# The first of eight column groups of a two-branch decoder layer takes three of its sixteen chunk pairs by seven block products instead of eight

## The chip, the cores and the metric

The kernel runs on one core of one Trainium2 chip. The metric is the device time of one execution in microseconds (us). The kernel before was timed three times: 1829.57, 1831.45 and 1831.59 us, median 1831.45.

## The reference

One layer, in fp32, on 256 tokens with 16 learned meta tokens ahead of them (272 rows of 4096):

```python
h = rmsnorm(x, norm_g)
p = h @ w_in                     # 4096 x 16384: q k v g_attn | b c h_conv z, 2048 columns each
o = stick_breaking_attention(heads(q), heads(k), heads(v))      # 16 heads of 128
o = group_rmsnorm(o * silu(g_attn), attn_norm_g, 16)
y = b_conv * short_conv(c_conv * h_conv, conv_w)                # width 3 along the positions
y = group_rmsnorm(y * silu(z_conv), conv_norm_g, 16)
hs = x + concatenate([o, y]) @ w_out                            # 4096 x 4096
return rmsnorm(hs, final_norm_g)[:, 16:]                        # the meta tokens are dropped
```

## The kernel before, in words

**Operands in two halves.** Every fp32 operand is split into a rounded high part and the rest: ScalarE (ACT) casts it (line 308, tiles `wh`), VectorE (DVE) subtracts (line 309, tiles `wl`). A block product on TensorE (PE) is then three matmuls: low x high, high x high, high x low (lines 340, 342, 343). The last of them needs the `wl` part.

**Pieces.** All work is a list `pieces`, written out at lines 93 to 121. Eight column groups `g` of two heads each come first. A group has two parts:
- sixteen *pairs* `j`. A pair is two chunks of 128 rows of `w_in` against the columns of q, g_attn, b and z: 1024 columns, in two halves of 512 columns. Two pieces of 512 KB, A and B, hold it. The 256 tokens are two halves of 128. Two chunks, two token halves and two column halves make eight block products of 512 columns each, 24 matmuls, which add up in four PSUM banks (D11, D21, D12, D22).
- 32 pieces "p" for k, v, c and h (line 332 and following: 24 matmuls of 272 columns each, or 258).

Three column blocks of the output product, which run like pairs, and a last stretch of "o" pieces follow the groups.

**Seven products.** For the pairs named in `SJ` (4, 6, 8, 10, 12, 14) the groups from 1 on take seven block products, a scheme of Winograd's kind: 21 matmuls. The pair then has four pieces, A B T U. T and U are no loads: DVE makes them from A and B (lines 319 to 321: two additions into a tile `t`, one into A's second half, one into A's first half, so U lies in A's own buffer), and they are split like a loaded piece. The token side needs four sums of token blocks per pair (`token_sums`, line 223: four operations on GpSimd (POOL), a cast by ACT at line 232, a subtraction by DVE at line 233). The products P1, P5, P7 and P6 collect in four more banks (4 to 7; the program names them P4, P5, P6 and P7 by their banks), and `evict_sums` (line 508) adds them into SBUF after pair 14. `evict` (line 522) then adds D11, D21, D12 and D22 at the end of the sixteen pairs.

**Group 0.** It takes all pairs by eight products. It is also where the tokens come in: with each A piece, `load_x` fetches two chunks of the transposed tokens (tile `xr`, 272 KB) and `prep_x` (line 205) scales them (ACT line 213, DVE line 211), splits them (ACT line 218, DVE line 219, tiles `xs`) and, for the pairs in `SJ`, makes the token sums, which groups 1 to 7 read. Nine more pieces "x" (512 KB of the tokens in their own layout) come after pairs 4 to 12, for the sum of squares by ACT (line 281). `evict` copies the four banks by ACT. When the group ends, `finish_stats` (line 410) works out the norm's factors: three small matmuls `ss_x` (lines 419 to 421) between DVE steps.

**Queues and rings.** Every engine takes its instructions strictly in its written order. Loads are issued by SyncE's queue (SP), also in order. Raw pieces have five buffers; a load is issued when a buffer is free, which for a plain piece is when DVE has made its low part, and for the A of a seven-product pair when U has been split. Split pieces have six buffers, freed by PE. A layer beneath the kernel puts each engine's instructions in order ahead of time. Banks 4 to 7 are handed out in turn to all that is not a D bank (`bank`, line 72): in group 0 before, to `warm`, `ss_x`, the first "p" block `mm0_0`, `qT0`, the second "p" block `mm0_1`, and so on.

Of the kernel before, what the change touches and what calls it, by code (L numbers as in the profile page):

```python
# [12 lines left out]
ALU = mybir.AluOpType  # L13
# [12 lines left out]
GROUPS = 8  # L26
# [14 lines left out]
SJ = (4, 6, 8, 10, 12, 14)  # L41
# [3 lines left out]
OUT_SJ = (8, 9, 10, 11, 12, 13)  # L45


def seven(g, j):
    return j in (OUT_SJ if g >= GROUPS else SJ if g else ())

# [4 lines left out]
def kernel(ctx, tc, xt, xin, xm, par, fg, w1, w2, out):  # L57
# [53 lines left out]
    for g in range(GROUPS, GROUPS + 3):  # L111
        for at_, j in enumerate(OUT_ORDER):
            for q in "ABTU" if seven(g, j) else "AB":
                pieces.append((q, g, j))
                if g == GROUPS and (at_, q) in ((2, "A"), (3, "A"), (9, "A")):
                    pieces.append(ms[{2: 4, 3: 5, 9: 6}[at_]])
        fin[g] = len(pieces) - 1
# [119 lines left out]
    def open_mix(g0):  # L237
        if g0 == 0:
            sctx.close()
        mixp = ctx.enter_context(tc.tile_pool(name=f"mixp{g0}", bufs=1))  # L240
        mixh.extend(mixp.tile([P, 4, SEQ], F32R, name=f"mixh{g}") for g in range(g0, g0 + 4))
        mixl.extend(mixp.tile([P, 4, SEQ], F32R, name=f"mixl{g}") for g in range(g0, g0 + 4))
# [4 lines left out]
    def load(i):  # L247
        p = pieces[i]
        if p[0] in "TU":
            return  # L250
        if p[:2] == ("A", 0) and p[2] > 0:
            load_x(p[2])
        t = wp.tile([P, 1024], F32, tag="raw", name=f"raw{i}", bufs=5)
        raws[i] = t
        if p[0] == "x":
            if p[1] < 8:
                r, c = divmod(p[1], 4)
                nc.sync.dma_start(out=t, in_=xin[r * P:(r + 1) * P, c * 1024:(c + 1) * 1024])
            else:
                nc.sync.dma_start(out=t[:, :512], in_=xm)  # L260
        elif p[0] == "m":
            nc.sync.dma_start(out=t.rearrange("p (a b) -> p a b", a=4), in_=mixd[p[1]])
        elif i < 2:
            for h in range(2):
                nc.sync.dma_start(out=t[:, 512 * h:512 * h + 512], in_=where[i][:, 512 * h:512 * h + 512])
                if i == 0 and h == 0:
                    nc.sync.dma_start(out=xr[0][:, 1:, :], in_=xt[:, 1:2, :])
        else:
            nc.sync.dma_start(out=t, in_=where[i])
# [55 lines left out]
    psum = {}  # L325
# [50 lines left out]
    def mm_in(i):  # L376
        p = pieces[i]
        if p[0] in "xm":
            return
        wh, wl = splits.pop(i)  # L380
        if p[0] == "p":
            _, (u, b), kc = p
            if kc == 0:
                psum[u, b, "p"] = bank(f"mm{u}_{b}")
            for kk in range(8):
                c = slice(kk * P, (kk + 1) * P)
                mm_k(psum[u, b, "p"], b, kc * 8 + kk, wh[:, c], wl[:, c])
            return
        for q, st, c in works(i)[p[0]]:
            key = p[1], q  # L390
            if key not in begun:
                psum[key] = bank(f"P{q}_{p[1]}", (q + 4) % 8 if p[1] == GROUPS + 1 else q)
            mm_p(key, p[2], st, wh[:, c], wl[:, c])
# [7 lines left out]
    def run_tasks(i):  # L401
        ready = [t for t in tasks if t[0] <= i]
        for t in ready:
            tasks.remove(t)
        for t in sorted(ready, key=lambda t: t[0]):
            t[1](*t[2])

    V, A, G, T = nc.vector, nc.scalar, nc.gpsimd, nc.tensor
# [85 lines left out]
    def plain_block(u, b, e):  # L494
        ps = psum.pop((u, b, "p"))
        if b == 0:
            k_block(u, ps[:, :L])
        elif b == 1:
            v_block(u, ps[:, :L], e + 4 if u % 2 == 0 else e + 2)
        elif b == 2:  # L500
            c_block(u, ps[:, META - 2:L])
        else:
            h_block(u, ps[:, META - 2:L], e + 1)
# [4 lines left out]
    def evict_sums(g):  # L508

        cq = wk.tile([P, 2, 512], F32, tag="cq", name=f"cq{g}")  # L510
        cb = wk.tile([P, 2, 512], F32, tag="cb", name=f"cb{g}")
        gr[g] = dict(cq=cq, cb=cb)
        if g == 0:
            return
        p1, p5, p7, p6 = (psum.pop((g, q)) for q in (P1, P5, P7, P6))
        A.copy(out=cq[:, 0], in_=p1)
        V.tensor_tensor(out=cb[:, 0], in0=p6, in1=cq[:, 0], op=ALU.add)
        V.tensor_tensor(out=cq[:, 1], in0=p7, in1=cb[:, 0], op=ALU.add)
        V.tensor_tensor(out=cb[:, 0], in0=p5, in1=cb[:, 0], op=ALU.subtract)
        V.tensor_tensor(out=cb[:, 1], in0=p5, in1=cq[:, 1], op=ALU.subtract)  # L520

    def evict(g):
        s = gr[g]
        for q, d in ((D11, s["cq"][:, 0]), (D21, s["cq"][:, 1]), (D12, s["cb"][:, 0]), (D22, s["cb"][:, 1])):
            if g:
                V.tensor_tensor(out=d, in0=psum.pop((g, q)), in1=d, op=ALU.add)
            else:
                A.copy(out=d, in_=psum.pop((g, q)))
        for c, q in (("cq", "h"), ("cb", "c")):
            v = s[c].rearrange("p t (u w x) -> p t u w x", u=2, w=2)  # L530
            s[q] = v[:, :, :, 0, :], v[:, :, :, 1, :]
# [162 lines left out]
    def open_tail():  # L694
        hd["w_out"] = True
        xctx.close()
        open_mix(4)
        tp = ctx.enter_context(tc.tile_pool(name="tp", bufs=1, side="right"))
        res.extend(tp.tile([P, D], F32, name=f"res{t}") for t in range(2))
        acc.extend(tp.tile([P, 1], F32, name=f"acc{t}") for t in range(2))  # L700
        sqs.extend(tp.tile([P, 1], F32, name=f"sq{t}") for t in range(2))
        fgs["pool"] = tp
        for q in range(4):
            tp.tile([P, 1024], F32R, tag=f"keep{q}", name=f"none{q}")
        tp.tile([P, 24], F32, name="pad_k")
# [4 lines left out]
    def load_res(nb):  # L710
        c, w = cols(nb)
        for t in range(2):
            nc.sync.dma_start(out=res[t][:, c:c + w], in_=xin[t * P:(t + 1) * P, c:c + w])
        f = fgs["pool"].tile([P, 512], F32, tag="fg", name=f"fg{nb}", bufs=2)
        nc.sync.dma_start(out=f[:, :w], in_=fg[:, c:c + w].broadcast_to([P, w]))
        fgs[nb] = f
# [86 lines left out]
    for i in range(1 - SPLITS, n):  # L803

        ahead = min(4, max(0, i - (n - 16) + 5))
        while loaded < min(i + LOADS + ahead + 1, n):
            load(loaded)
            loaded += 1
        while halved < min(i + SPLITS + ahead + 1, n):
            split(halved)  # L810
            halved += 1
        if i < 0:
            continue
        p = pieces[i]
        if i < n1:
            mm_in(i)
            if p[0] == "p" and p[2] == 3:
                plain_block(*p[1], i)
            if p[0] == ("U" if p[1] else "B") and p[2] == SJ[-1]:
                evict_sums(p[1])  # L820
                if p[1] == GROUPS - 1:
                    open_mix(0)
            if i in fin.values():
                evict(pieces[i][1])
            if i == n1 - 1:
                open_tail()
        elif p[0] in "ABTU":
            mm_in(i)
            g = p[1]
            if p[0] == "B" and p[2] in (2, 3):  # L830
                load_res(2 * (g - GROUPS) + p[2] - 2)
            if p[0] == "U" and p[2] == OUT_SJ[-1]:
                out_sums(g)
            if i == fin[g]:
                for q, nb, t in ((D11, 0, 0), (D12, 1, 0), (D21, 0, 1), (D22, 1, 1)):
                    psum["o", 2 * (g - GROUPS) + nb, t] = psum.pop((g, q))
                for nb in range(2):
                    for t in range(2):
                        out_block(2 * (g - GROUPS) + nb, t)
        elif p[0] == "o":  # L840
            if "all" not in hd:
                hd["all"], turn[0] = True, 4
            _, nb, kc = p
            final = nb == 8
            mm_out(i, (0,) if final else (0, 1))
            if kc == 3:
                load_res(nb)
            if kc == (15 if nb < 7 else 7):
                for t in (0,) if final else (0, 1):
                    out_block(nb, t)  # L850
        run_tasks(i)
# [75 lines left out]
```

## Time and profile before

| what | us |
|---|---|
| median of three runs | 1831.45 |
| the profiled execution | 1830.19 |
| its span, from first to last instruction | 1828.5 |
| sixteen pairs of group 0 on PE | 7.28 to 94.64 |
| pair 10 and pair 11 of group 0 | 61.99 to 72.88 |
| pair 12 and pair 13 | 72.88 to 83.75 |
| pair 14 and pair 15 | 83.75 to 94.64 |

Times in the trace count from the start of the span. "busy" of a matmul row is longer than the step from one matmul to the next, since matmuls overlap; the steps are read from the starts. A row that ends in x2 merges two equal instructions.

### The profile page before, as it was taken

Reading aid. Unit: us, or ns where it says so; the run is one execution under the profiler, and the core shown is the slowest. Engines: PE = TensorE matmul, PEld = TensorE weight load, DVE = VectorE, ACT = ScalarE, POOL = GpSimd, SP = SyncE. Lnnn points to the kernel's source line nnn. Section 1 sums busy time; section 2 is a strip of 40 time slices with the busy share of each in tenths; the row PEclk is TensorE's granted clock in tenths of the full one; section 3 lists DMA queues with packets and bytes.
Section 4 is the critical chain, followed back from the end, with each engine's and each line's share of the span. In section 5 each row is a group of like instructions: output and inputs, shape, how many; then the busy total and the mean of one; then the engine's idle time right before and its main releaser. Section 6 shows DMA issues by size and latency. Waiting matters only on the chain.

```text
span 1828.5 us, 29350 instructions
## 1 busy us (share of the span) xinstructions
PE 1809.9 (99%) x11142; PEld 1635.4 (89%) x11142; DVE 1332.4 (73%) x1993; ACT 1067.8 (58%) x1638; POOL 120.6 (7%) x168
## 2 busy tenths in 40 slices
PE   9999999999999999999999999999999999999997
PEld 7899889988998899889988998899889978888887
DVE  6776687668766866686668666866686779998953
ACT  7766556655665566556655665566556655555542
POOL 1210001000100010001000100010001021000000
PEclk9999999999999999999999999999999999999999
DMA  8864566556655665565556555664565676766763
GB/s 316 296 214 168 166 214 198 171 171 215 200 167 170 215 198 167 172 214 199 172 169 214 198 170 171 212 202 166 175 217 187 206 266 201 233 223 194 231 214 117
DMA packets 106846, 364.26 MB, mean 199 GB/s; under 512 B 11984, under 2 KB 16848, under 8 KB 106704
## 3 DMA queue, kind: packets, MB, share of 16 engines
q1 hardware_dynamic: 102672, 358.72, 59.8%
q10 hardware_dynamic: 4032, 3.67, 0.6%
q8 instruction: 87, 1.43, 0.3%
q14 instruction: 55, 0.45, 0.1%
HBM read 354.48 MB, written 7.86 MB: 198 GB/s over the span
## 4 chain that ended last, share of the span: by engine, by line
PE 97%; ACT 1%; DVE 1%; POOL 1%; issue 0%; DMA 0%; DVEq 0%; SPq 0%; ACTq 0%
PE P L343 16%; PE P L340 16%; PE P L342 16%; PE mm L332 14%; PE mm L333 13%; PE mm L334 13%; PE mo L752 2%; PE mo L751 2%; PE mo L750 2%; PE z L602 0%; PE po L648 0%; PE mxc L570 0%; PE z L601 0%; PE po L644 0%; ACT wh L308 0%
## 5 line engine op out<-in xcount | busy, mean ns | idle before, releaser
L309 DVE TENSOR_TENSOR wl<-raw,wh 128x1024 fp32r<-128x1024 f32 (+1 forms) x700 | 810.4, 1179 | 279.7 <-ACT wh L308 277.1
L308 ACT CAST wh<-raw 128x1024 fp32r<-128x1024 f32 (+1 forms) x700 | 691.5, 1010 | 548.6 <-PE mm L333 194.4
L332 PE MATMUL mm<-xs,wh 128*128 128x258 f32 (+1 forms) x2048 | 587.8, 287 | 0.0
L333 PE MATMUL mm<-xs,wh 128*128 128x258 f32 (+1 forms) x2048 | 581.7, 284 | 0.0
L334 PE MATMUL mm<-xs,wl 128*128 128x258 f32 (+1 forms) x2048 | 581.6, 284 | 0.0
L332 PEld LDWEIGHTS mm<-xs,wh 128*128 128x128 f32 x2048 | 385.6, 188 | 2.8
L333 PEld LDWEIGHTS mm<-xs,wh 128*128 128x128 f32 x2048 | 385.7, 188 | 0.9
L334 PEld LDWEIGHTS mm<-xs,wl 128*128 128x128 f32 x2048 | 385.8, 188 | 0.0
L340 PE MATMUL P<-wh,xs 128*128 128x512 f32 x814 | 318.1, 391 | 1.5 <-ACT wh L308 1.5
L343 PE MATMUL P<-wl,xs 128*128 128x512 f32 x814 | 316.9, 389 | 0.0
L342 PE MATMUL P<-wh,xs 128*128 128x512 f32 x814 | 316.7, 389 | 0.0
L340 PEld LDWEIGHTS P<-wh,xs 128*128 128x128 f32 x814 | 152.8, 188 | 32.8 <-ACT wh L308 1.8
L343 PEld LDWEIGHTS P<-wl,xs 128*128 128x128 f32 x814 | 152.8, 188 | 32.1 <-DVE wl L309 0.3
L342 PEld LDWEIGHTS P<-wh,xs 128*128 128x128 f32 x814 | 152.9, 188 | 31.1
L343 PE MATMUL P<-wl,mixh 128*128 128x512 f32 x294 | 115.2, 392 | 0.3 <-DVE wl L309 0.3
L340 PE MATMUL P<-wh,mixl 128*128 128x512 f32 x294 | 115.1, 392 | 0.0
L342 PE MATMUL P<-wh,mixh 128*128 128x512 f32 x294 | 115.0, 391 | 0.0
L309 DVE TENSOR_TENSOR wl<-t,wh 128x1024 fp32r<-128x1024 f32 x60 | 73.4, 1223 | 19.0 <-ACT wh L308 19.0
L319 DVE TENSOR_TENSOR t<-raw,raw 128x512 f32<-128x512 f32 x120 | 79.1, 688 | 10.2 <-DMA raw<-w 9.7
L308 ACT CAST wh<-t 128x1024 fp32r<-128x1024 f32 x60 | 63.1, 1052 | 29.7 <-ACT wh L308 13.3
L343 PEld LDWEIGHTS P<-wl,mixh 128*128 128x128 f32 x294 | 55.6, 189 | 12.1 <-DVE wl L309 0.7
L340 PEld LDWEIGHTS P<-wh,mixl 128*128 128x128 f32 x294 | 55.6, 189 | 11.5
(243 smaller groups left out, 1796.1 us busy)
## 6 DMA issues: line engine op xcount, KB each, us to landing
raw<-w SPq DMA_DIRECT2D x638, 512.0 KB, 4.0
raw<-xin SPq DMA_DIRECT2D x8, 512.0 KB, 5.4
xr<-xt SPq DMA_DIRECT2D x15, 272.0 KB, 5.3
raw<-mixd SPq DMA_DIRECT2D x7, 512.0 KB, 4.0
res<-xin SPq DMA_DIRECT2D x14, 256.0 KB, 5.5
out<-res SPq DMA_DIRECT2D x4, 512.0 KB, 3.4
mixd<-mfh ACTq DMA_DIRECT2D x14, 128.0 KB, 2.9
mixd<-mfc ACTq DMA_DIRECT2D x14, 128.0 KB, 4.9
```

Source lines behind the costliest of these rows:

```text
L308: nc.scalar.copy(out=h[:, c], in_=t[:, c])
L309: nc.vector.tensor_tensor(out=lo[:, c], in0=t[:, c], in1=h[:, c].bitcast(F32), op=ALU.subtract)
L319: nc.vector.tensor_tensor(out=s[:, c], in0=a[:, c], in1=t[:, 512:], op=ALU.add)
L332: nc.tensor.matmul(out=o, lhsT=h, rhs=x[:, 0, s:], start=k == 0, stop=False)
L333: nc.tensor.matmul(out=o, lhsT=h, rhs=x[:, 1, s:], start=False, stop=False)
L334: nc.tensor.matmul(out=o, lhsT=lo, rhs=x[:, 0, s:], start=False, stop=k == KC - 1)
L340: nc.tensor.matmul(out=o, lhsT=a[1], rhs=h, start=key not in begun, stop=False)
L342: nc.tensor.matmul(out=o, lhsT=a[0], rhs=h, start=False, stop=False)
L343: nc.tensor.matmul(out=o, lhsT=a[0], rhs=lo, start=False, stop=last)
L750: T.matmul(out=o, lhsT=ml, rhs=h, start=m == 0, stop=False)
L751: T.matmul(out=o, lhsT=mh, rhs=h, start=False, stop=False)
L752: T.matmul(out=o, lhsT=mh, rhs=lo, start=False, stop=m == UNITS - 1)
```

## The change

`seven` names pairs 10, 12 and 14 (the last three of `SJ`) for group 0 too. Their pieces become A B T U there, and their matmuls go from 24 to 21. `evict_sums` and `evict` do in group 0 what they do in the other groups: one ACT copy and four DVE operations after pair 14, and four DVE additions in place of four ACT copies at the end. `prep_x` is not touched: the token sums were made in group 0 already, and pairs 10, 12 and 14 now read them there.

```diff
 def seven(g, j):
-    return j in (OUT_SJ if g >= GROUPS else SJ if g else ())
+    return j in (OUT_SJ if g >= GROUPS else SJ if g else SJ[-3:])
...
     def evict_sums(g):
...
         gr[g] = dict(cq=cq, cb=cb)
-        if g == 0:
-            return
         p1, p5, p7, p6 = (psum.pop((g, q)) for q in (P1, P5, P7, P6))
...
     def evict(g):
         s = gr[g]
         for q, d in ((D11, s["cq"][:, 0]), (D21, s["cq"][:, 1]), (D12, s["cb"][:, 0]), (D22, s["cb"][:, 1])):
-            if g:
-                V.tensor_tensor(out=d, in0=psum.pop((g, q)), in1=d, op=ALU.add)
-            else:
-                A.copy(out=d, in_=psum.pop((g, q)))
+            V.tensor_tensor(out=d, in0=psum.pop((g, q)), in1=d, op=ALU.add)
...
-            if p[0] == ("U" if p[1] else "B") and p[2] == SJ[-1]:
+            if p[0] == "U" and p[2] == SJ[-1]:
                 evict_sums(p[1])
```

The change also moves instructions, since the layer beneath puts them in order anew. Lines from 513 on have numbers lower by 2, and from 526 on by 5, in the changed kernel. The number behind a tile's letters is its piece: in the changed kernel 26 to 29 are A, B, T and U of pair 10, 31 and 32 pair 11, 34 to 37 pair 12, 39 and 40 pair 13, 41 to 44 pair 14, 45 and 46 pair 15, and 47 is the first "p" piece.

On DVE, from the low part of pair 10's B piece on, before (`xr11` are the tokens of pair 11):

```order
L309 TENSOR_TENSOR wl27_620<-raw27_565,wh27_619 128x1024
L211 TENSOR_SCALAR xr11_586<-xr11_586,pt_84 128x272
L219 TENSOR_TENSOR xs5_129<-xr11_586,xs5_129 128x2x272
L309 TENSOR_TENSOR wl29_647<-raw29_588,wh29_646 128x1024
L309 TENSOR_TENSOR wl30_665<-raw30_617,wh30_664 128x1024
```

And now:

```order
L309 TENSOR_TENSOR wl27_614<-raw27_565,wh27_613 128x512
L319 TENSOR_TENSOR t27_617<-raw26_543,raw27_565 128x512 x2
L211 TENSOR_SCALAR xr11_622<-xr11_622,pt_84 128x272
L320 TENSOR_TENSOR raw26_543<-raw26_543,t27_617 128x512
L321 TENSOR_TENSOR raw26_543<-raw27_565,raw26_543 128x512
L309 TENSOR_TENSOR wl28_627<-t27_617,wh28_626 128x1024
L219 TENSOR_TENSOR xs5_129<-xr11_622,xs5_129 128x2x272
L309 TENSOR_TENSOR wl29_645<-raw26_543,wh29_644 128x1024
L309 TENSOR_TENSOR wl31_672<-raw31_624,wh31_671 128x1024
L309 TENSOR_TENSOR wl32_685<-raw32_642,wh32_684 128x1024
L211 TENSOR_SCALAR xr12_663<-xr12_663,pt_84 128x272
```

Four additions and two more splits stand ahead of pair 11's splits, and the scaling of pair 12's tokens (`xr12`) stands behind all of them.

On PE in pair 12, from the T piece on, now (before, every product's three matmuls stood together, piece after piece):

```order
L340 MATMUL P5_0_692<-wh36_737,sum12_140 128x512
L342 MATMUL P5_0_692<-wh36_737,sum12_140 128x512
L340 MATMUL P6_0_696<-wh36_737,sum12_140 128x512
L342 MATMUL P6_0_696<-wh36_737,sum12_140 128x512
L340 MATMUL P2_0_219<-wh37_755,xs6_130 128x512
L343 MATMUL P5_0_692<-wl36_738,sum12_140 128x512
L343 MATMUL P6_0_696<-wl36_738,sum12_140 128x512
L342 MATMUL P2_0_219<-wh37_755,xs6_130 128x512
```

The first matmul of the U piece, which reads its high part `wh37`, stands ahead of the two that read T's low part; pair 14 has the same order.

On PE at the end of group 0, before:

```order
L343 MATMUL P3_0_227<-wl40_827,xs7_131 128x512
L419 MATMUL ss_x_946<-eight_98,rep_942 128x16
L420 MATMUL ss_x_946<-ident_93,rep_942 128x128
L421 MATMUL ss_x_946<-ident_93,rep_942 128x128
L332 MATMUL mm0_0_991<-xs0_124,wh41_844 128x272
```

And now:

```order
L343 MATMUL P3_0_227<-wl46_888,xs7_131 128x512
L332 MATMUL mm0_1_1169<-xs0_124,wh51_957 128x272
L333 MATMUL mm0_1_1169<-xs0_124,wh51_957 128x272
L332 MATMUL mm0_0_1030<-xs0_124,wh47_899 128x272
L333 MATMUL mm0_0_1030<-xs0_124,wh47_899 128x272
L334 MATMUL mm0_0_1030<-xs0_124,wl47_900 128x272
```

Two matmuls of the second "p" block, with the high part of piece 51, now stand ahead of the first block's, whose first piece is 47; `ss_x` stands 44 matmuls further on. `mm0_0` lies in bank 6, which the P7 product holds until `evict_sums` has read it.

On DVE, that reading (line 516, from `P6_0`) has this place now:

```order
L309 TENSOR_TENSOR wl48_909<-raw48_863,wh48_908 128x1024
L309 TENSOR_TENSOR wl49_921<-raw49_885,wh49_920 128x1024
L515 TENSOR_TENSOR cb0_931<-P7_0_718,cq0_930 128x512
L309 TENSOR_TENSOR wl50_940<-raw50_897,wh50_939 128x1024
L516 TENSOR_TENSOR cq0_930<-P6_0_696,cb0_931 128x512
L309 TENSOR_TENSOR wl51_958<-raw51_906,wh51_957 128x1024
```

It stands behind the splits of pieces 47 to 50. After this stretch, apart from numbers, the order on PE and SP is that of before.

## The prediction

> **What bounds the kernel now.** The profile's page comes first: busy shares, and the chain that ended last.
>
> ```profile
> PE 1809.9 (99%) x11142; PEld 1635.4 (89%) x11142; DVE 1332.4 (73%) x1993; ACT 1067.8 (58%) x1638; POOL 120.6 (7%) x168
> PE 97%; ACT 1%; DVE 1%; POOL 1%; issue 0%; DMA 0%; DVEq 0%; SPq 0%; ACTq 0%
> ```
>
> PE bounds the kernel, so a matmul less is worth its step, as long as PE finds its operands ready. Whether it does in group 0 is the question. PE's waits in the first 130 us, and the engines' busy time in pairs 10 and 11, 12 and 13, 14 and 15:
>
> ```profile
> PE P L340 <- ACT wh L308: 1.5, 1, 1.5
> PE warm L84 <- DVE ones L81: 1.1, 1, 1.1
> ```
> ```profile
> 61.99:72.88 10.89, 10.89 (x50) 9.01 (x49) 7.19 (x11) 8.35 (x14) 2.26 (x4) 1.00 0.93 331
> 72.88:83.75 10.87, 10.87 (x49) 9.01 (x48) 7.96 (x13) 7.22 (x12) 3.12 (x4) 1.00 0.81 284
> 83.75:94.64 10.89, 10.89 (x50) 9.01 (x49) 10.65 (x27) 7.54 (x10) 0.00 (x0) 1.00 0.75 246
> ```
>
> The columns are PE, PEld, DVE, ACT, POOL, the granted clock, the DMA share and GB/s. PE waits nowhere after its first piece. But DVE is busy for 7.2 to 10.7 us of each 10.9, and ACT for 7.2 to 8.4. The starts on PE, then on DVE, say how much lead there is.
>
> ```profile
> 61.99 0.39 PE L340 MATMUL P<-wh,xs 128*128 128x512 f32 x1
> 72.88 0.39 PE L340 MATMUL P<-wh,xs 128*128 128x512 f32 x1
> ...
> 95.22 0.37 PE L332 MATMUL mm<-xs,wh 128*128 128x272 f32 x1
> ...
> 95.55 0.28 PE L334 MATMUL mm<-xs,wl 128*128 128x272 f32 x1
> 95.67 0.29 PE L332 MATMUL mm<-xs,wh 128*128 128x272 f32 x1
> ```
> ```profile
> 60.31 2.36 DVE L309 TENSOR_TENSOR wl<-raw,wh 128x1024 fp32r<-128x1024 f32 x2 [0.26 <-ACT wh L308]
> ...
> 66.94 0.35 DVE L211 TENSOR_SCALAR xr<-xr,pt 128x272 f32<-128x272 f32 x1
> 67.21 0.15 DVE L413 TENSOR_REDUCE sst<-sq 128x1 f32<-128x4 f32 x1
> ...
> 71.60 2.36 DVE L309 TENSOR_TENSOR wl<-raw,wh 128x1024 fp32r<-128x1024 f32 x2 [0.26 <-ACT wh L308]
> ...
> 75.01 0.73 DVE L219 TENSOR_TENSOR xs<-xr,xs 128x544 fp32r<-128x544 f32 x1 [0.70 <-ACT xs L218]
> ...
> 77.38 1.22 DVE L309 TENSOR_TENSOR wl<-raw,wh 128x1024 fp32r<-128x1024 f32 x1
> 78.51 0.98 DVE L219 TENSOR_TENSOR xs<-xr,xs 128x544 fp32r<-128x544 f32 x1
> 81.47 0.69 DVE L233 TENSOR_TENSOR sum<-sf,sum 128x512 fp32r<-128x512 f32 x1 [1.98 <-ACT sum L232]
> 82.08 0.47 DVE L417 TENSOR_SCALAR rep<-ones,sst 128x128 f32<-128x128 f32 x2
> ```
>
> From 61.99 to 72.88 are 48 matmuls: 0.227 us each. A split takes 1.22 us, and its successor starts after 1.14 (two take 2.36). The low part of pair 10's A is there at 60.31 + 1.22 = 61.53; PE reads it two matmuls after 61.99, at 62.44: a lead of 0.9 us. Pair 12's A is ready at 72.82 and read at 73.33: 0.5. PE never waits, but group 0 has half a microsecond to spare, not the length of a queue.
>
> **The change part by part.** *Removed*: 3 x 3 matmuls of 0.227 us, 0.68 a pair, 2.04 us in all. *Added*, on DVE, from group 1, where seven products run already, and on ACT, there and in group 0:
>
> ```profile
> 237.67 1.29 DVE L319 TENSOR_TENSOR t<-raw,raw 128x512 f32<-128x512 f32 x2
> ...
> 241.75 0.68 DVE L320 TENSOR_TENSOR raw<-raw,t 128x512 f32<-128x512 f32 x1
> ```
> ```profile
> 59.23 1.99 ACT L308 CAST wh<-raw 128x1024 fp32r<-128x1024 f32 x2
> ...
> 77.55 0.65 ACT L218 CAST xs<-xr 128x544 fp32r<-128x544 f32 x1 [0.25 <-DVE xr L211]
> 80.82 0.62 ACT L232 CAST sum<-sf 128x512 fp32r<-128x512 f32 x1 [2.63 <-POOL sf L231]
> ```
>
> An addition takes 0.68 us, 0.60 to its successor; I take the same for a split of 512 columns. A cast takes 1.05, 0.95 to its successor. I walk the new order with these, from 60.31 on, where nothing has changed yet.
>
> *Pair 10.* DVE: A 60.31, B 61.45, `t` 62.05 to 63.3, scaling of pair 11's tokens to 63.5, two additions (each waits for the one before) to 64.9, T's split to 66.0, token split (0.65) to 66.7, U's split until 67.9. PE without a wait would read U's low part after 17 matmuls, at 61.99 + 3.86 = 65.85. It is 2.04 us late there, 0.68 are saved: pair 10 ends 1.36 us later than before, at 68.80. Pair 11 follows: its splits end at 69.0 and 70.2, before PE reads them.
>
> *Pair 12.* The scaling of its tokens (L211) stands behind those splits on DVE and ends at 70.4 (in the run shown it started at 66.94). The token sums on POOL wait for it:
>
> ```profile
> 67.62 0.47 POOL L228 TENSOR_TENSOR sf<-xr 128x128 f32<-128x128 f32 x1 [8.95 <-ACT xr L213]
> ...
> 69.50 0.46 POOL L231 TENSOR_TENSOR sf<-xr,sf 128x128 f32<-128x128 f32 x1
> ...
> 77.59 1.33 POOL L228 TENSOR_TENSOR sf<-xr 128x128 f32<-128x128 f32 x1 [7.63 <-DVE xr L211]
> 78.88 0.94 POOL L229 TENSOR_TENSOR sf<-xr 128x128 f32<-128x128 f32 x1
> 79.78 0.46 POOL L230 TENSOR_TENSOR sf<-sf,xr 128x128 f32<-128x128 f32 x1
> 80.32 0.47 POOL L231 TENSOR_TENSOR sf<-xr,sf 128x128 f32<-128x128 f32 x1
> ```
>
> The four took 2.34 us for pair 12 and 3.20 for pair 14, where DVE's split at 77.38 and subtraction at 78.51 ran beside them. In the new order a split and a subtraction stand beside them in pair 12 too, so I take 3.20: POOL until 73.8, ACT's cast of the sums (0.62) to 74.4, DVE's subtraction (0.69) to 75.1. All that follows on DVE stands behind it: B 75.7, `t` 76.9, scaling, additions to 78.6. ACT then casts U to 79.7. PE wants that cast 13 matmuls into the pair, at 68.80 + (24 + 13) x 0.227 = 77.2: 2.47 late. Lateness after pair 12: 1.36 - 0.68 + 2.47 = 3.15. [...]
>
> *Pair 14* repeats this. DVE: U of pair 12 to 81.5, pair 13's two splits to 83.8, scaling to 84.1; POOL to 87.4, sums to 88.8, B 89.4, `t` 90.6, scaling of the last tokens, additions to 92.35; ACT's cast of U to 93.4. Pair 13 ends at 86.9, PE wants the cast at 89.9: 3.54 late. Lateness 3.15 - 0.68 + 3.54 = 6.0; pair 15 ends at 100.7, against 94.64.
>
> *The end of the group.* PE first wants piece 51's high part, then bank 6. Loads, on the page and in the stretch from 83 to 100 us:
>
> ```profile
> raw<-w SPq DMA_DIRECT2D x638, 512.0 KB, 4.0
> ```
> ```profile
> raw<-w SPq DMA_DIRECT2D x10, 512.0 KB, 4.8
> ```
>
> Piece 49 gets a buffer only when pair 14's U or A is split, at 95.3; with 4.0 it lands at 99.3, is cast at 100.4 and split by 101.6. Behind it on DVE stand line 515 (0.6), piece 50's split (1.14) and line 516 (0.68): bank 6 is free at 104.0. Piece 51, loaded from 97.6 on, is cast by 102.7. PE could have begun `mm0_0` at 100.7 + 0.25. Another 3.1 us late: 9.1 in all. With 4.8 it would be 0.8 more.
>
> *Covered, taken at nothing.* The other two of the four operations of `evict_sums` and `evict`'s four additions (6 x 0.6 us, in place of ACT copies) and piece 51's split stand between line 516 and the two L417 operations (0.47) that `ss_x` waits for: ready near 109.1. PE comes to `ss_x` 44 matmuls of 0.12 us after 104.0, at 109.3; what goes over that is lost one for one. The squares of x, loads and tables keep their number. After this stretch PE bounds again and nothing gives the lateness back; by the page's 97% there is no other chain to hide it behind.
>
> **Sum**: 2.04 + 2.47 + 3.54 + 3.1 of waits, less 2.04: 9.1 us on the profiled execution's 1830.2 (1828.5 of span), so 1839.3. That execution lies 1.3 below the median of the three runs and inside their spread of 2.0. A difference under 0.2% (3.7 us) is about what a measurement of this kernel can't tell from no change.
>
> **The rivals.** *Hidden.* Splits run ahead as in the other groups, and PE gains all nine matmuls: 1830.2 - 2.04 = 1828.2, which counts as the same. For it: PE waits nowhere in the groups that use six such pairs. Against it: the lead of 0.9 us in pair 10, where U needs 2.04 more. It decides from a lead of about 3 us at pair 10's A. 0.06, and 0.02 more that the time falls by over 0.2%.
>
> *Only the pairs pay.* Buffers come free sooner than I walk, the end of the group adds nothing, and POOL keeps 2.34: 9.1 - 3.1 - 1.7 = 4.3, so 1834.5. For it: splits of the "p" pieces need one split for 24 matmuls. Against: line 516 stands behind pieces 49 and 50. 0.12, and another 0.05 that less than 3.7 is left.
>
> *The clock falls.* PE idles in pieces of about 0.4 to 2 us between 88 and 104. If the granted clock halved for the 32 matmuls that end pair 14 and make pair 15, these would take 7.3 us longer: 1846.6. Against it stands PE's wait of 1.5 us ahead of its first piece; the clock, the column of ones before the DMA share, stayed at 1.00:
>
> ```profile
> 5.80:7.30 1.50, 0.02 (x1) 0.02 (x1) 1.14 (x4) 1.49 (x5) 0.00 (x0) 1.00 0.94 319
> 7.30:10.00 2.70, 2.70 (x12) 2.25 (x13) 2.47 (x5) 2.05 (x4) 0.00 (x0) 1.00 0.99 349
> ```
>
> [...] 0.06.
>
> My forecast has the remaining 0.69. That the change does nothing is excluded by the order: nine matmuls fewer on PE, 23 rows more on DVE.
>
> **How the numbers follow.** The range goes down to *only the pairs pay* less half the spread of the runs, 1833.5. Upward it takes the 4.8 us load and a quarter of a microsecond (the idle time before the split at 60.31) at each of some ten hand-overs between engines, and half the spread: 9.1 + 0.8 + 2.5 + 1.0, 1843.6; I take 1844. Faster 0.02; same 0.06 + 0.05 = 0.11; slower 0.87.
>
> **What would show it.** Right: PE waits on line 340 in pairs 10, 12 and 14 of 2, 2.5 and 3.5 us, released by `wl` or `wh`; POOL's first operation for pair 12 starts near 70.6 and not 67.6; `mm0_0` starts near 104 (95.22 before); group 1 the same but later. Wrong: PE without waits before 105 us, or pair 15 ending before 97; or a granted clock below 1.00 there.

## The result, and the profile after

The changed kernel's median is 1840.99 us (1840.77, 1841.21, 1837.35, 1841.72); on the same chip the kernel before took 1830.67 (four runs). The ratio is 1.0052, 95% interval 1.0040 to 1.0064: slower, by 10.3 us where 9.1 were forecast. The profiled execution took 1840.77 us, its span 1839.1.

First the busy shares and the chain that ended last, from the page of the changed kernel:

```profile
PE 1813.4 (99%) x11133; PEld 1636.4 (89%) x11133; DVE 1346.7 (73%) x2019; ACT 1071.1 (58%) x1641; POOL 122.6 (7%) x168
...
PE 93%; DVE 2%; DMA 1%; ACT 1%; issue 1%; POOL 1%; SPq 0%; DVEq 0%; ACTq 0%; POOLq 0%
```

PE has its nine matmuls less (11133 for 11142), DVE has 26 instructions more (2019 for 1993; the forecast counted 23, and nothing in its sum hangs on that). PE's share of the chain fell from 97% to 93%. These 4% are not the loss: the chain now meets a wait of PE at 104 us and runs ahead of it through loads, casts and splits instead of PE. Where PE waits, its list for the first 140 us says (us in total, times, the longest):

```profile
PE P L340 <- ACT wh L308: 4.4, 5, 1.3
PE mm L332 <- ACT wh L308: 3.2, 1, 3.2
PE warm L84 <- DVE ones L81: 1.1, 1, 1.1
PE P L343 <- DVE wl L309: 0.9, 1, 0.9
PE P L340 <- DVE sum L233: 0.6, 1, 0.6
```

Only the 1.1 us and the first part of the 4.4 (PE's first piece, 1.0 us) were there before. The rest lies in group 0: inside the pairs, and one wait of 3.2 us at the end of the group. The stretches pairs 10 and 11, 12 and 13, 14 and 15, and the end (columns PE, PEld, DVE, ACT, POOL, clock, DMA share, GB/s):

```profile
62.91:74.99 12.08, 11.09 (x46) 8.22 (x45) 10.50 (x15) 8.38 (x12) 3.65 (x4) 1.00 0.75 242
74.99:87.53 12.54, 10.85 (x46) 8.22 (x45) 11.72 (x16) 9.00 (x14) 3.44 (x4) 1.00 0.80 270
87.53:100.97 13.44, 11.10 (x46) 8.03 (x44) 12.65 (x16) 8.70 (x10) 0.05 (x1) 1.00 0.46 157
100.97:105.00 4.03, 0.81 (x6) 0.64 (x6) 3.28 (x5) 2.54 (x3) 0.00 (x0) 1.00 0.99 380
```

Before, each took 10.87 to 10.89 us, and DVE was busy for 7.2 to 10.7 of them. Now they take 12.08, 12.54 and 13.44 with fewer matmuls, and DVE is busy for 10.5 to 12.7: it has become the slower engine. A stretch of 45 matmuls (21 + 24) without any wait takes 10.20 us (a run below shows it), so the three lose 7.5 us and keep 5.4 of loss after the 2.04 saved. The list of waits shows less, 4.9 us (4.4 + 0.9 + 0.6 - 1.0), since it counts from the modelled end of the matmul before, 0.39 us after its start, where the next one starts after 0.227 us if nothing is waited for. The start of pair 12 shows what DVE waits for. POOL, then DVE:

```profile
70.12 0.93 POOL L229 TENSOR_TENSOR sf<-xr 128x128 f32<-128x128 f32 x1 [10.84 <-ACT xr L213]
71.29 1.44 POOL L228 TENSOR_TENSOR sf<-xr 128x128 f32<-128x128 f32 x1 [0.24 <-DVE sst L413]
72.81 0.82 POOL L230 TENSOR_TENSOR sf<-sf,xr 128x128 f32<-128x128 f32 x1
73.71 0.46 POOL L231 TENSOR_TENSOR sf<-xr,sf 128x128 f32<-128x128 f32 x1
```
```profile
70.64 0.57 DVE L211 TENSOR_SCALAR xr<-xr,pt 128x272 f32<-128x272 f32 x1
...
71.20 1.21 DVE L309 TENSOR_TENSOR wl<-raw,wh 128x1024 fp32r<-128x1024 f32 x1
72.33 0.98 DVE L219 TENSOR_TENSOR xs<-xr,xs 128x544 fp32r<-128x544 f32 x1
74.85 0.69 DVE L233 TENSOR_TENSOR sum<-sf,sum 128x512 fp32r<-128x512 f32 x1 [1.54 <-ACT sum L232]
```

The same subtraction in the kernel before:

```profile
70.65 0.69 DVE L233 TENSOR_TENSOR sum<-sf,sum 128x512 fp32r<-128x512 f32 x1 [1.55 <-ACT sum L232]
```

The scaling stands near where the walk put it (70.64; 70.1 was forecast). POOL begins at 70.12 with line 229, which waits for ACT alone; line 228, which the forecast had first, waits for DVE's scaling. POOL ends at 74.17 (73.8), and DVE stands idle for 1.54 us until ACT has cast the sums. The idle time itself was there before (1.55). New is that the sums come 3.3 us later, counted from the start of pair 10, and that pair 12's B split and its additions are queued behind. At the end of the group, ACT, DVE and PE:

```profile
101.06 1.04 ACT L308 CAST wh<-raw 128x1024 fp32r<-128x1024 f32 x1 [1.15 <-DMA raw<-w]
103.26 1.04 ACT L308 CAST wh<-raw 128x1024 fp32r<-128x1024 f32 x1 [1.16 <-DMA raw<-w]
```
```profile
101.08 0.68 DVE L515 TENSOR_TENSOR cb<-P,cq 128x512 f32<-128x512 f32 x1
102.13 1.23 DVE L309 TENSOR_TENSOR wl<-raw,wh 128x1024 fp32r<-128x1024 f32 x1 [0.37 <-ACT wh L308]
103.28 0.69 DVE L516 TENSOR_TENSOR cq<-P,cb 128x512 f32<-128x512 f32 x1
```
```profile
104.36 0.40 PE L332 MATMUL mm<-xs,wh 128*128 128x272 f32 x1 [3.22 <-ACT wh L308]
```

Line 516 ends at 103.97 (104.0 was forecast), and piece 51's cast, which the first matmul moved to the front reads, runs from 103.26 to 104.30. Either would hold PE, and the cast came last: pair 15's last matmul would have been followed at 100.97, and `mm0_1` starts at 104.36.

The accounts: pairs +1.19, +1.67 and +2.55, 5.4 together; the end of the group 3.4; a stretch of half clock behind it, shown below, about 1.7: 10.5. In this execution pair 10 began 0.9 us later than in the one before: PE's first matmuls, from 6.8 to 10.3 us, step 0.43 us, where they step 0.23 in the kernel before. Between 120 us and the end 0.8 came back, where the forecast had nothing come back. Most of it are two waits of PE that only the kernel before has, 0.4 us at line 658 (between 170 and 215 us) and 0.3 at line 343 (between 1515 and 1605). That makes the 10.6 us between the spans.

### The profile page after: what moved, and what is told of

The parts are those of the page before. It is cut to its first block, busy times and chain, and to the rows that moved or that the text cites. A ratio compares the mean times of both kernels' runs of the same rounds, so it can differ in the third digit from the quotient of the medians.

```text
span 1839.1 us, 29372 instructions
## 1 busy us (share of the span) xinstructions
PE 1813.4 (99%) x11133; PEld 1636.4 (89%) x11133; DVE 1346.7 (73%) x2019; ACT 1071.1 (58%) x1641; POOL 122.6 (7%) x168
## 3 DMA queue, kind: packets, MB, share of 16 engines
q8 instruction: 87, 1.43, 0.3%
## 4 chain that ended last, share of the span: by engine, by line
PE 93%; DVE 2%; DMA 1%; ACT 1%; issue 1%; POOL 1%; SPq 0%; DVEq 0%; ACTq 0%; POOLq 0%
PE P L340 15%; PE P L343 15%; PE P L342 15%; PE mm L332 14%; PE mm L333 13%; PE mm L334 13%; PE mo L746 2%; PE mo L745 2%; PE mo L747 2%; DVE wl L309 1%; DMA raw<-w 1%; DMA raw<-xin 1%; ACT wh L308 0%; PE z L597 0%; DVE t L319 0%
## 5 line engine op out<-in xcount | busy, mean ns | idle before, releaser
L340 PE MATMUL P<-wh,xs 128*128 128x512 f32 x799 | 313.7, 393 | 1.9 <-ACT wh L308 1.9
L342 PE MATMUL P<-wh,xs 128*128 128x512 f32 x799 | 311.6, 390 | 0.0
L343 PE MATMUL P<-wl,xs 128*128 128x512 f32 x799 | 311.2, 391 | 0.1
L340 PEld LDWEIGHTS P<-wh,xs 128*128 128x128 f32 x799 | 150.5, 188 | 33.5 <-ACT wh L308 3.1
L342 PEld LDWEIGHTS P<-wh,xs 128*128 128x128 f32 x799 | 150.6, 188 | 30.5
L309 DVE TENSOR_TENSOR wl<-t,wh 128x1024 fp32r<-128x1024 f32 x63 | 77.2, 1225 | 18.9 <-ACT wh L308 18.9
L319 DVE TENSOR_TENSOR t<-raw,raw 128x512 f32<-128x512 f32 x126 | 82.8, 687 | 6.2 <-DMA raw<-w 5.6
L340 PE MATMUL P<-wh,sum 128*128 128x512 f32 x180 | 70.6, 392 | 3.2 <-ACT wh L308 2.5
L343 PE MATMUL P<-wl,sum 128*128 128x512 f32 x180 | 69.9, 390 | 0.9 <-DVE wl L309 0.9
```

The costliest lines, as they stand in the source:

```text
L309: nc.vector.tensor_tensor(out=lo[:, c], in0=t[:, c], in1=h[:, c].bitcast(F32), op=ALU.subtract)
L319: nc.vector.tensor_tensor(out=s[:, c], in0=a[:, c], in1=t[:, 512:], op=ALU.add)
L340: nc.tensor.matmul(out=o, lhsT=a[1], rhs=h, start=key not in begun, stop=False)
L342: nc.tensor.matmul(out=o, lhsT=a[0], rhs=h, start=False, stop=False)
L343: nc.tensor.matmul(out=o, lhsT=a[0], rhs=lo, start=False, stop=last)
```

## The experiments

Of the changed kernel unless said otherwise. Medians stand beside the kernel before on the same chip: 1830.6 for `e1_banks`, `e2_pair10`, `e3_no_adds` and `e4_no_pool`, 1830.87 for `e5_pair14`, `e6_less`, `e8_no_x` and `e9_no_both`, 1830.55 for the last two. "Six pairs" is the time on PE from the start of pair 10 to the end of pair 15: 32.65 us before, 38.1 after.

My theory: PE now waits for one serial chain on DVE, which the token sums (DVE, POOL, ACT, DVE) and the additions both lengthen, and then once more for bank 6 and piece 51. Rivals: one of the two parts alone sets the loss; the squares of x (loads and ACT work beside the pairs) set it; the end of the group is late anyway; PE was short of lead even for plain pairs.

### The end of the group alone: banks 4 and 6 exchanged for the first two "p" blocks

```diff
             turn[0] += 1
+            i = {"mm0_0": 4, "mm0_1": 6}.get(nm, i)
```

> The changed kernel, with banks 4 and 6 exchanged between the first two p blocks of group 0: mm0_0 lies in bank 4, which one ACT copy frees, and mm0_1 in bank 6. PE then begins with mm0_0 and no longer with two matmuls of mm0_1. The walk (the loss is DVE's chain inside pairs 10, 12 and 14, then a wait at the end of the group): the pairs lose what they lose in the changed kernel, 5.4 us from the start of pair 10 to the end of pair 15, the wait of 3.2 us at the end goes, and with it the 3.4 us at half clock that cost 1.7 us: 5 us less than the changed kernel, some 1836. Rival, loads (PE waits because loads come late, and the end is only where it shows): the wait moves to mm0_0's own pieces and the time stays within 1.5 us of the changed kernel.

Measured: 1836.99 us, ratio 1.0033 (1.0020 to 1.0045), 4.0 less than the change. The last matmul of pair 15, and `mm0_0` right behind it:

```profile
101.06 0.39 PE L344 MATMUL P<-wl,xs 128*128 128x512 f32 x1
101.28 0.29 PE L333 MATMUL mm<-xs,wh 128*128 128x272 f32 x1
```

The wait is gone, and 4 us with it; later ones of 0.3 to 0.5 us took its place. The end-of-group term was real. What made it was the busy bank and the matmul order built around it: with the banks exchanged `mm0_0` stands first again. This run takes both away at once; that the bank alone is enough, pair 14 alone shows below.

### One pair at a time

Pair 10 alone by seven products (`FIRST = (10,)`), and pair 14 alone (`FIRST = (14,)`):

```diff
-    return j in (OUT_SJ if g >= GROUPS else SJ if g else SJ[-3:])
+    return j in (OUT_SJ if g >= GROUPS else SJ if g else FIRST)
...
```

Beside that, `evict_sums` runs after pair 14 in both.

> Only pair 10 of group 0 by seven products; evict_sums runs after pair 14 as in the changed kernel. The walk: pair 10 ends 1.2 us later than before, net of the 0.68 that it saves; pair 12's token scaling still stands behind pair 10's U split, so its sums and all that DVE does behind them come some 3 us later than before and pair 12 or 13 waits 1 to 2 us more; no wait at the end of the group. 2 to 4 us over the kernel before, 1833 to 1835. Rival, the end of the group is the whole loss: within 1 us of the kernel before.

> Only pair 14 of group 0 by seven products. PE's order at the end of the group is mm0_0 first, then mm0_1, but mm0_0 still lies in bank 6, which line 516's operation frees behind four splits of p pieces. The walk: pairs 10 to 13 as in the kernel before; pair 14 wants U's cast 1.3 us before it is there and saves 0.7, so it ends 0.6 later; then a wait of 2 to 3 us for bank 6 at the end of the group, which may halve the clock for 3.4 us (1.7 us more). 2.5 to 5 us over the kernel before, 1833 to 1836. Rival, the pairs are the loss and the end is not: within 1 us of the kernel before.

Measured: pair 10 alone 1831.42 (1.0004, 0.9994 to 1.0013), pair 14 alone 1834.97 (1.0023, 1.0014 to 1.0032). The first two stretches of the first (its third is 10.88 again), and the third of the second:

```profile
63.45:75.94 12.49, 11.06 (x46) 8.21 (x45) 10.91 (x16) 8.77 (x13) 3.65 (x4) 1.00 0.75 241
75.94:86.82 10.88, 10.88 (x49) 9.01 (x48) 10.16 (x17) 8.87 (x14) 2.82 (x4) 1.00 0.94 323
```
```profile
83.75:96.31 12.56, 11.10 (x46) 8.03 (x44) 12.28 (x16) 8.29 (x10) 0.00 (x0) 1.00 0.52 173
```

Pair 10 costs 1.6 us net by itself, and plain pairs behind it run at full speed: I had expected a second delay in pair 12, and it did not come. The trace shows the 1.6 but the time rose by 0.8 only, and no change lies inside its interval. Pair 14 alone costs 1.67 and not the 0.6 that I gave it, and its end of the group waits 2.6 us for bank 6 (`mm0_0` at 99.03, released by the operation that reads `P6_0`, line 517 here): the wait at the end needs only this one pair, and no matmul moved to the front.

### Without the additions, without POOL, without both

Group 0's additions (lines 319 to 321) left out, T and U split from A; the four POOL operations for pairs 10, 12 and 14 left out; and both:

```diff
             a = sums.pop(("A",) + p[1:])
+            if p[1] == 0:
+                sums[("T",) + p[1:]], sums[("U",) + p[1:]] = a, a
+                return
```
```diff
+        if j in (10, 12, 14):
+            f = t.rearrange("p a (b c) -> p a b c", b=2)
+            d = dst.rearrange("p h (a b) c -> p h a b c", a=2)
+            nc.scalar.copy(out=d[:, 0], in_=f)
+            nc.vector.tensor_tensor(out=d[:, 1], in0=f, in1=d[:, 0].bitcast(F32), op=ALU.subtract)
+            return
```

> The changed kernel without the four additions on DVE that make T and U in group 0: T and U are split straight from A, so group 0's numbers are not the reference's. Loads, casts, splits, token sums and the hold on A's buffer until U is split stay. The walk: DVE's chain per pair is 2.6 us shorter; pair 10 has no wait and ends 0.7 us earlier than before, pairs 12 and 14 wait about 1 us each; PE's order at the end of the group is again mm0_0 first. Within 2 us of the kernel before, 1829 to 1833. Rival, loads (the held buffer and the loads behind it are the limit): less than 2 us are won on the changed kernel, over 1838.

> The changed kernel with POOL's four operations left out for pairs 10, 12 and 14 in group 0: blocks of the tokens stand in the place of their sums, so the products' numbers are not the reference's in any group that reads them. Cast and subtraction of the sums stay on ACT and DVE. The walk: pair 10 loses what it does in the changed kernel (1.2 us), pairs 12 and 14 lose 2 to 4 us less together, since B's split no longer stands behind 3.2 us on POOL; the end of the group keeps its wait, as mm0_1 still stands first there. 1837 to 1839. Rival, the additions alone are the loss: within 1 us of the changed kernel.

> The changed kernel without the four additions per pair and without POOL's four operations for pairs 10, 12 and 14 in group 0 (neither T and U nor the token sums hold the reference's numbers). Casts, splits, loads, banks and evict_sums stay. With either of the two alone left out, the six pairs took 0.2 us more than in the kernel before. If the loss inside the pairs is one serial chain, in which the additions and POOL stand one behind the other, both out leave PE nothing to wait for and the six pairs take 2.0 us less than in the kernel before, 30.6 us; the time stays at 1829 to 1832 if a wait of 1 to 2 us for bank 6 remains at the end. Rival, they only hide behind each other (each wait covers another of the same length): the six pairs stay within 0.5 us of the kernel before.

Measured: no additions 1832.14 (1.0008, 0.9998 to 1.0017); no POOL 1836.45 (1.0032, 1.0021 to 1.0042); neither 1829.66 (0.9996, 0.9987 to 1.0006). The stretches of the three kernels in this order:

```profile
63.49:73.70 10.21, 10.21 (x46) 8.34 (x45) 7.24 (x11) 8.03 (x14) 2.25 (x4) 1.00 0.93 311
73.70:85.45 11.75, 10.80 (x46) 8.30 (x46) 11.65 (x17) 9.28 (x15) 3.47 (x4) 1.00 0.80 276
85.45:96.33 10.88, 10.51 (x46) 8.18 (x44) 10.66 (x12) 8.88 (x11) 0.00 (x0) 1.00 0.73 254
```
```profile
61.70:71.90 10.20, 10.20 (x46) 8.45 (x45) 10.03 (x18) 8.46 (x14) 0.00 (x0) 1.00 0.83 274
71.90:83.23 11.33, 10.79 (x46) 8.29 (x45) 11.33 (x18) 8.46 (x12) 0.00 (x0) 1.00 0.90 291
83.23:94.60 11.37, 10.80 (x46) 8.10 (x44) 11.37 (x15) 8.06 (x10) 0.00 (x0) 1.00 0.56 200
```
```profile
62.10:72.30 10.20, 10.20 (x46) 8.45 (x45) 9.24 (x21) 9.41 (x16) 0.00 (x0) 1.00 0.93 328
72.30:82.50 10.20, 10.20 (x46) 8.45 (x45) 10.17 (x23) 9.06 (x12) 0.00 (x0) 1.00 0.84 302
82.50:92.70 10.20, 10.20 (x46) 8.45 (x45) 9.55 (x11) 6.85 (x9) 0.00 (x0) 1.00 0.86 283
```

Either part left out takes the six pairs from 38.1 to 32.8 or 32.9 us; both left out, to 30.60, the full 2.04 below 32.65. The two effects do not add: about 5.2 each alone, 7.5 together. In two chains side by side, both together could lose no more than the larger of them alone, 2.3 us, and they lose 7.5. One chain that may be some 3 us longer before PE waits (5.2 + 5.3 - 7.5) fits all three. The sizes are not quite pure, since the layer beneath orders the instructions anew in each kernel. The first came out in time as expected, the second a little under its 1837 to 1839. Without POOL, pair 10 has no loss at all, where I had expected it to keep 1.2: POOL's sums delay pair 10's splits too. Even the kernel with neither is only 1.2 us faster than before (with no difference inside the interval), for a wait of 0.9 us at `ss_x` is left, which comes late behind the evictions:

```profile
PE ss_x L428 <- DVE cb L527: 0.9, 1, 0.9
```

So this is about what the three pairs bring in this group, if additions and sums cost nothing; without that last wait it would be the 2.04.

### The lead of the plain pairs: the kernel before without nine matmuls

```diff
...
+            if p[1] == 0 and p[2] in (10, 12, 14) and p[0] == "A" and q == D22:
+                continue
```

> The kernel before with nine matmuls of group 0 left out and nothing else changed: in pairs 10, 12 and 14 the product of A's second half with the second token half is not made, so group 0's numbers are not the reference's. PE has what the change gives it, at no cost on any other engine. The walk (group 0's preparation of tokens and splits has a lead of 0.5 us, so PE can't use more): pair 12 starts 0.7 us earlier, pairs 12 and 14 start with waits of 0.2 to 0.7 us, in all 1.0 to 1.4 us are won of 2.04. Rival, PE alone bounds group 0: no waits, 2.04 us are won.

Measured: 1829.59 (0.9992, 0.9982 to 1.0001), 1.28 us less than the kernel before, with no difference just inside the interval. The first two stretches took 10.20 each, the third 10.47:

```profile
83.69:94.16 10.47, 10.47 (x46) 8.37 (x45) 10.23 (x27) 7.14 (x9) 0.00 (x0) 1.00 0.73 232
```

The six pairs take 30.87: 1.78 of 2.04 won in this execution, where the lead of half a microsecond had let me expect 1.0 to 1.4. That does not show that DVE follows a faster PE, for this execution came to pair 10 with more lead. Its first matmuls step 0.43 us up to 10.3 us, as in the changed kernel's, and PE began pair 10 at 63.29, 1.30 us later than in the kernel before; DVE began the split of pair 10's A only 0.41 us later:

```profile
60.72 2.36 DVE L309 TENSOR_TENSOR wl<-raw,wh 128x1024 fp32r<-128x1024 f32 x2 [0.26 <-ACT wh L308]
```

That is 0.9 us more lead. From there DVE keeps the pace of the kernel before: the split of pair 14's A starts at 82.99, where it starts at 82.47 there. And PE does not hold DVE back: of the waits of DVE and ACT from 55 to 95 us in the kernel before, 0.2 us are put down to PE. Without the gift pair 14 would have been late by some 0.8 us more (my estimate, 1.30 - 0.52), and about 1.0 us won. So the run supports the half microsecond of lead.

The same holds for the other runs. From the start of DVE's split of pair 10's A to PE's start of pair 10 it is 1.68 us in the kernel before, 2.00 in the changed kernel, 1.26 in `e1_banks` and 2.13 in `e3_no_adds`; sums over the six pairs can differ by some half a microsecond for that alone.

### Without three of the x pieces

The pieces "x" after pairs 10, 11 and 12 left out:

```diff
-            if g == 0 and 4 <= j < 13:
+            if g == 0 and 4 <= j < 10:
...
```

> The changed kernel without the x pieces after pairs 10, 11 and 12: 1.25 MB less to load, and no squares by ACT there; the sums of squares of those columns are ones, so the norm's factors are not the reference's. The walk: DVE's chain is as long as before, so the pairs lose what they lose in the changed kernel within 1 us, and PE's order at the end still has mm0_1 first, but piece 51's number is now 48 and its load is no earlier: within 2 us of the changed kernel, 1839 to 1842. Rival, loads and ACT bound the stage: 1836 or less.

Measured: 1839.55 (1.0049, 1.0034 to 1.0064); the six pairs take 38.4 us, and the wait at the end is 2.9. Three loads less (two of 512 KB, and the last piece, which has 256) and their ACT work less change nothing: the changed kernel itself, run again, took 1839.55 too (below). That rival falls.

### The token sums of pairs 12 and 14 sooner

The banks exchanged as above, and scaling and POOL sums of pair 12's and 14's tokens written ahead of pair 11's and 13's splits:

```diff
...
+        if p in (("A", 0, 11), ("A", 0, 13)):
+            scale_x(p[2] + 1)
```

> The changed kernel with banks 4 and 6 exchanged for the first two "p" blocks (as in the run that did this alone, 1836.99 us) and, beside that, the token scaling and POOL sums of pairs 12 and 14 written one pair earlier, so that DVE's scaling of those tokens stands one split sooner. The theory of one serial chain through DVE and POOL: POOL's first operation for pair 12 starts about 1.1 us sooner, pairs 12 and 14 each lose 1.1 to 2.2 us less, the six pairs take about 36 us instead of 38.1, no wait stands at the end of the group: 1833 to 1836. It doesn't go under the kernel before, since the additions still stand in the chain. The rival, that POOL's place in the chain hardly counts and the additions alone set the loss: six pairs at 38 us and 1836 to 1838.

Measured: 1838.29 (1.0037, 1.0024 to 1.0050), no better than the exchanged banks alone. The three pair-to-pair stretches are 14.00, with 1.7 us of half clock in it, 12.23 and 13.46. DVE in pair 12:

```profile
74.26 0.69 DVE L252 TENSOR_TENSOR sum<-sf,sum 128x512 fp32r<-128x512 f32 x1 [2.38 <-ACT sum L251]
...
75.21 1.83 DVE L330 TENSOR_TENSOR wl<-raw,wh 128x1024 fp32r<-128x1024 f32 x2 [0.19 <-ACT wh L329]
```

The subtraction of the sums came 0.6 us sooner than in the change (74.26 for 74.85), but in the new order the split of pair 12's own A (the first of the two in the 1.83) stands behind it, where it had filled the gap before: DVE's idle time grew from 1.54 to 2.38 us. Without the half clock the six pairs took 38.0 us, as the rival has it; the time lies 0.3 above its range, and 2.3 above mine. But the run does not show that POOL's place is without effect, as the rival has it: `e4_no_pool` says otherwise, and here what was gained was spent on the same engine. It tells only that this move is not enough.

### The clock: the changed kernel again

> The changed kernel itself once more, for the clock. The theory that PE's waits at the end of group 0 halve the clock for one 3.41 us window or more, by where the windows fall in that run: 1837 to 1842 us, the mean clock lower by 0.001 for each 1.7 us, and in the profiled run a half-clock window right after the one in which PE idles for most of the time, and none if the waits fall on two windows with about half each. The rival, that the clock fell for another reason (its place in the program): the half-clock window begins at the same place, 105 to 106 us, as before.

Measured: 1839.55 (1.0044, 1.0029 to 1.0059). The records of the granted clock change at steps of 3.41 us; the stretches below are cut there. First the profiled execution after the change, then this one (the seventh number is the clock):

```profile
99.01:102.42 3.41, 2.12 (x10) 1.43 (x8) 2.98 (x4) 1.94 (x2) 0.00 (x0) 1.00 0.86 310
102.42:105.83 3.41, 1.47 (x12) 1.47 (x13) 3.03 (x4) 2.10 (x2) 0.00 (x0) 1.00 1.00 400
105.83:109.25 3.42, 3.42 (x18) 3.42 (x17) 3.42 (x7) 0.03 (x1) 0.00 (x0) 0.50 0.80 308
```
```profile
99.81:103.22 3.41, 2.17 (x10) 1.47 (x8) 2.92 (x4) 1.75 (x2) 0.00 (x0) 1.00 0.82 286
103.22:106.64 3.42, 2.07 (x16) 2.07 (x17) 3.42 (x5) 2.10 (x2) 0.00 (x0) 1.00 1.00 392
106.64:110.05 3.41, 3.41 (x30) 3.41 (x29) 3.41 (x9) 1.05 (x1) 0.00 (x0) 1.00 0.85 329
```

The same kernel waits about 3 us at the same place in both. In the first, most of the wait falls into one stretch, where PE is busy for 1.47 of 3.41 us, and the next runs at half clock: 18 matmuls in place of 30. In the second it is spread over two stretches (2.17 and 2.07 busy), and the clock stays. That is what the theory of the windows expected; the rival, a fixed place in the program, falls. The mean clock is 0.996 in both, as the second has its window of half clock elsewhere, right behind PE's wait of 2.2 us for its first piece:

```profile
4.24:7.65 3.41, 1.21 (x10) 0.97 (x9) 1.90 (x5) 2.95 (x5) 0.00 (x0) 1.00 0.95 277
7.65:11.06 3.41, 3.41 (x10) 2.64 (x9) 2.48 (x5) 2.15 (x5) 0.00 (x0) 0.50 1.00 374
```

There the matmuls step 0.43 us. In the changed kernel's first execution they step 0.43 us up to 10.3 us as well; its records of the clock begin only there, and where there is none the column shows 1.00.

## Why the prediction was right, and where it was not

**Right: the sign, the places and most of the sizes.** The net loss of the three pairs was forecast as 1.36, 1.79 and 2.85 us and came as 1.19, 1.67 and 2.55; the wait at the end as 3.1 and came as 3.4. `ss_x` costs nothing in the changed kernel, as forecast. That it is one chain with token sums and additions in it is shown by leaving out each and both; that the end of the group is a separate term, by the exchange of the banks.

**Right in sum, not in each step.** The walk had one wait in each pair, on line 340 in pairs 12 and 14. Each pair has two or three, first for a part of T or for the token sums and then for U; in pair 10 the longest, 0.9 us, is on line 343 for T's low part. At the end of the group the walk had piece 51 cast by 102.7 and bank 6 free last, at 104.0. Bank 6 was free at 103.97 and the cast came last, at 104.30: the load of piece 51 took 5.5 us (97.64 to 103.2 in the chain), where 4.0 were taken. That mis-sized load cost only 0.3 us because bank 6 was nearly as late. Times on the trace that agree, as 103.97 with 104.0, agree in part by luck: pair 10 began 0.9 us later than the walk has it, and counted from there line 516 ended after 41.1 us, where the walk has 42.0.

**Wrong: the clock.** The forecast gave 0.06 to a fall of the clock. It fell, for one stretch of 3.41 us, worth half of that, 1.7 us. The sum had this term at nothing, and the term is more than the 10.3 - 9.1 = 1.2 by which it was short; the pairs and the end came to 8.8 of the 9.1. Which of the other three executions had it, no trace shows; their mean clocks are 0.995, 0.997 and 0.994, and the one with 0.997 is the fastest, 1837.35. No single wait filled the stretch ahead of the fall: of the 3.2 us at the end of the group 1.94 lay in it (102.42 to 104.36), and PE was busy for the other 1.47. In `e10_early` two waits together took that time, neither of them over 1.3 us:

```profile
63.65:67.06 3.41, 1.78 (x8) 0.85 (x6) 3.38 (x6) 2.77 (x4) 0.00 (x0) 1.00 0.82 255
67.06:70.47 3.41, 3.41 (x8) 2.69 (x9) 3.41 (x5) 3.38 (x6) 0.11 (x1) 0.50 0.54 192
```

Of two profiled runs of one kernel the first had the wait mostly in one window of 3.41 us (1.47 busy), the second about evenly in two (2.17 and 2.07), and only the first had half clock behind it. PE was busy for 0.65 to 1.78 us in windows that were followed by half clock. The row that was to speak against the rival, PE's wait of 1.5 us at 5.8, did not decide it: the wait lay across two windows, in which PE was busy for 2.95 and 2.34 us. In `e2_pair10`, `e3_no_adds` and `e11_again` the wait at the same place was 2.0 to 2.2 us, and a window of half clock followed. The fall was also smaller than the rival made it (1.7 us for 7.3), and in the changed kernel's profile it came behind pair 15, not in it.

**Right: "half a microsecond to spare".** The kernel before without nine matmuls won 1.78 us over the three in its profiled execution, but 0.8 to 0.9 of lead came from a late start of PE there; DVE did not go faster. The time of all its runs, 1.28 us less, lies in the range expected from the lead, and its interval is too wide to decide.

**Right for a part that was not named: pair 10.** The walk charged pair 10's loss to the additions alone. Without the four POOL operations pair 10 has no loss either (10.20 us). The walk began at 60.31 with that delay already in it, so the number came out, but its cause was told incompletely.

**The rivals.** *Hidden* is excluded by the waits. *Only the pairs pay* gave 1834.5; with the wait at the end removed the kernel took 1836.99, so the end was a cost of its own, but POOL kept its longer price (3.65 us in the first stretch and 3.44 in the second, where 2.26 and 3.12 us stand before).

**No version beats the kernel before.** The best with the reference's result is pair 10 alone, level with it. By the run with neither additions nor sums about 1.2 us are to be had where additions and sums cost nothing. More raw buffers, with which pieces 49 to 51 could be loaded sooner, were not tried.

## What to carry to other kernels

A product saved on a bound engine is worth its step only if the engine that makes its operands has that much time free in the same stretch (here DVE was busy for 10.5 to 12.7 us of each, and the 2.04 us saved became 5.4 lost); where two helper chains (sums on POOL, additions on DVE) pass through one in-order queue, walk them as one chain and don't add their prices (about 5.2 us each alone, 7.5 together). A buffer that a new user holds at the end of a stage (bank 6) can reorder what comes next and cost nearly as much as the stage itself (3.4 us and the half clock behind it, for 5.4 in the pairs); changing which bank the next block takes was worth 4 us. A wait of PE had a second price where it left PE busy for 1.47 of the 3.41 us of one window: the next window ran at half clock, 1.7 us.

## What the runs showed of the hardware

**Half clock behind windows of 3.41 us that PE filled for 0.65 to 1.78.** In the eleven profiled runs beside the one before, from the first record of the clock up to 1400 us, the windows that PE had filled for 1.47, 1.73, 1.32, 0.65 and 1.78 us of 3.41 were each followed by one window at 0.50 (the change, `e1_banks`, `e4_no_pool`, `e8_no_x`, `e10_early`), and so were those filled for 1.43, 1.31 and 1.21 us at PE's first piece (`e2_pair10`, `e3_no_adds`, `e11_again`). The longest idle one, in `e8_no_x`, and the one behind it:

```profile
100.74:104.16 3.42, 0.65 (x5) 0.65 (x6) 2.77 (x4) 2.05 (x3) 0.00 (x0) 1.00 1.01 364
104.16:107.57 3.41, 3.41 (x17) 3.41 (x17) 3.41 (x6) 0.64 (x1) 0.00 (x0) 0.50 1.02 377
```

and one that kept the clock, in `e5_pair14`:

```profile
94.73:98.14 3.41, 1.74 (x8) 1.12 (x6) 2.38 (x3) 1.85 (x2) 0.00 (x0) 1.00 0.91 346
98.14:101.55 3.41, 2.52 (x20) 2.49 (x20) 3.41 (x6) 1.30 (x2) 0.00 (x0) 1.00 0.99 383
```

It was busy for 1.74 us, less than the 1.78 that were followed by half clock, and `e1_banks` has two windows of 1.73 us, of which one kept the clock (5.36:8.77) and one did not (77.04:80.45). By this column the two kinds of windows part between 1.73 and 1.78 us, and not sharply. Windows with 1.80 us (`e4_no_pool`, 4.69:8.10), 1.89 (`e11_again`, 89.57:92.98) and more kept the clock. Ahead of the first records the column does not part them: the window ahead of the steps of 0.43 us in the change (3.43:6.84, counted back from its first record at 10.26) was filled for 2.39 us, more than the 2.34 of the one in the kernel before (6.21:9.62) that has steps of 0.23 behind it. Whether what counts is busy time or something near it stays open.

**POOL beside DVE.** One of the 128 x 128 operations took 0.46 us alone and 0.82 to 1.44 beside DVE's splits and subtractions (the rows from 70.12 on). There it ended 0.32 us after an instruction of DVE had ended: at 72.73, after the split that ends at 72.41, and at 73.63, after the subtraction that ends at 73.31. The four took 4.0 us with their gaps from first to last, where the walk had 3.20 for them without the wait for DVE's half of the tokens. The longest is one in `e8_no_x`, beside a split, a token subtraction, three splits and another token subtraction, which fill DVE without a gap up to 83.70:

```profile
78.33 5.70 POOL L229 TENSOR_TENSOR sf<-xr 128x128 f32<-128x128 f32 x1 [5.37 <-ACT xr L214]
```

It ended at 84.03, 0.33 us after the last of them. So such an operation ended behind one instruction of DVE, as above, or only behind the sixth; why, these rows do not show.
